# A 32x32 triangular solve fed by block transposes on VectorE in place of trips through DRAM

## The chip, the cores and the metric

The kernel runs on one core of one Trainium2 chip. The metric is the device time of one execution in microseconds; of several executions the median is taken. The engines are TensorE (PE, with its weight loads as PEld), VectorE (DVE), ScalarE (ACT), GpSimd (POOL) and SyncE (SP). SyncE, ScalarE and GpSimd also issue DMAs.

## The reference

One decoder block on 1024 tokens with 1024 channels: an RMS norm, one wide input projection, two token mixers side by side (a mixture of three dilated sliding-window attentions, and a gated DeltaNet), SiLU and sigmoid gates, an output projection, the residual and a last norm. The change lies in the DeltaNet mixer, which works on 8 heads with chunks of 64 tokens:

```python
k_beta = kc * bc[..., None]
a = jnp.einsum('bhnid,bhnjd->bhnij', k_beta, kc) * decay_strict
eye = jnp.eye(c, dtype=a.dtype)
t_inv = lax.linalg.triangular_solve(eye + a, jnp.broadcast_to(eye, a.shape),
                                    left_side=True, lower=True, unit_diagonal=True)
u = t_inv @ (vc * bc[..., None])
w = t_inv @ (k_beta * jnp.exp(G)[..., None])
```

So for each head and each chunk a unit lower triangular matrix of 64x64 is inverted: 8 heads x 16 chunks = 128 matrices. The inverses give u and w, which a scan over the chunks then uses. All of this is in float32.

## The kernel before

**What fills the time.** Most of the work is the projections. They are cut into units of weight columns (attention, DeltaNet, gate, up), and each unit is a generator that issues three float16 matmuls per step (lines 183 to 185). A class `Feed` holds the units. TensorE's order is written out by hand: the code of a stage issues its own small matmuls and calls `feed.tick(n)` between them, and each tick puts one step of a unit into TensorE's queue. So TensorE always has projections to do while another engine prepares the next small step. If a small step is not ready when TensorE comes to it, TensorE waits, because its queue runs in order.

**The other engines.** The order of VectorE, ScalarE, GpSimd and SyncE is not written by hand. A planner lays it out ahead of time by priorities and by its own estimates of durations, and each engine then runs its queue in that fixed order. `tc.high_priority()` moves instructions ahead (evictions of PSUM banks), and the solve is traced with an offset of `-SOLVE_LATER` (1500), so that it is put behind other work and fills gaps. Weight loads are DMAs that GpSimd issues (`load_w`, line 162). ScalarE makes the high half of each weight block (line 166), and VectorE the low half (line 83, `wlo`).

**Buffers.** Tiles with the same tag share their buffers. In the pool `p2_` the tags `As`, `X` and `T1p` have one buffer each. Tag `As` holds As, T1 and later a load of `kbt`; tag `X` holds X and later another load of `kbt`; tag `T1p` holds T1p and also the staging tile `kd` of `spill_keys`.

**The solve.** The heads are worked in two groups `hb` of four. For each group a tile `MT[hb]` of [128, 8, 2, 2, 64] holds 32 pairs (n) of 64x64 matrices: 128 partitions are two chunks of 64 rows, so four blocks `kb` of 32 rows, and b = kb % 2 says which half of a chunk. The diagonal 32x32 blocks are inverted by substitution on VectorE, and TensorE's `merge` makes the off-diagonal block from them. The steps:

- `keys_side(hb)` (lines 1275 to 1303) normalises the keys, packs two scale vectors into `pack`, forms the products of the keys in `pairs` (the results go to `MT[hb]`), and calls `spill_keys`. Then it writes the four diagonal blocks of `MT` to a DRAM tile `m_d`, with rows and matrices exchanged. It transposes `pack` on TensorE (line 1294), copies it on ScalarE, and sends it through DRAM to `bsc`, one scale vector per matrix.
- `solve(hb)` (lines 1305 to 1337) loads `As` from `m_d`, so that each of the 128 partitions holds one 32x32 block (partition = kb, n). VectorE scales it, and 31 steps of two instructions each build the inverse in `X`. `T1` is minus X with its two block indices exchanged. `X` and `T1` go to DRAM (`u_d`, `t_d`) and come back with partitions exchanged: `X` into the diagonal blocks of `MT[hb]`, and `T1` into `T1p`.
- `merge(hb)` (lines 1339 to 1382) has TensorE multiply `T1p` with the off-diagonal block (line 1350), VectorE scale the result to Y, and TensorE multiply by the other diagonal block (line 1365); ScalarE copies that back to `MT` (line 1372). `MERGE_TICKS` = 5 ticks stand between the parts.
- `state_parts(hb)` loads `rvt` and `kbt` and forms u and w (lines 1413 and 1417).

The order is: `decay`, `keys_side` and `solve` of group 0, the same of group 1, then `state_side(0)` (merge and state of group 0), the query pairs of group 0 (line 1266), `state_side(1)`, and the query pairs of group 1. After them comes the scan over the chunks (from line 1672), which starts near 781 us.

Of the kernel before, what the change touches and what calls it, by code (L numbers as in the profile page):

```python
# [77 lines left out]
def hybrid_block(ctx: ExitStack, tc: tile.TileContext, A):  # L78
# [1097 lines left out]
    def heads_h2(x):  # L1176
        return x.rearrange("p t (q e) -> p t e q", e=2)
# [97 lines left out]
    def keys_side(hb):  # L1275
        hsl = slice(4 * hb, 4 * hb + 4)
        sumsq(hb, kT, kss, keep_keys)
        rnorm(rk[:, :, hsl], kss, 1.0)
        TT(brk[:, :, hsl], rk[:, :, hsl], beta[:, :, hsl], ALU.mult)
        TT(bgk[:, :, hsl], brk[:, :, hsl], eG[:, :, hsl], ALU.mult)  # L1280
        pack = p2_.tile([128, 2, 8, 4], F32, name="pack", tag="pack", bufs=2)
        packs.append(pack[:, 0].rearrange("p t h -> p (t h)"))
        for i, x in enumerate((brk, rk)):
            V.tensor_copy(pack[:, i].rearrange("p t (e q) -> p t e q", e=2), heads_h2(x[:, :, hsl]))
        pairs(hb, kT, MT[hb])
        spill_keys(hb)
        m_d = tc.dram_tile([4, 32, 32, 32], F32, name=f"m_d{hb}")
        for kb in range(4):
            b = kb % 2
            nc.sync.dma_start(out=m_d[kb].rearrange("n j i -> j n i"),  # L1290
                              in_=MT[hb][32 * kb:32 * kb + 32].rearrange("p t e q i -> p (t e q) i")[:, :, 32 * b:32 * b + 32])
        feed.tick(4)
        pp = bank("G", 2)
        PE.transpose(pp[0:64, 0:128], pack.rearrange("p a t h -> p (a t h)"), ident)
        packT = p2_.tile([64, 128], F32, name="packT", tag="packT", bufs=1)
        SC.copy(packT, pp[0:64, 0:128])
        sc_d = tc.dram_tile([2, 4, 32, 32], F32, name=f"sc_d{hb}")
        for i in range(2):
            nc.sync.dma_start(out=sc_d[i].rearrange("k n i -> n k i"),
                              in_=packT[32 * i:32 * i + 32].rearrange("p (k i) -> p k i", i=32))  # L1300
        bsc = p2_.tile([128, 2, 32], F32, name="bsc", tag="bsc", bufs=2)
        nc.sync.dma_start(out=bsc, in_=sc_d.rearrange("a k n i -> (k n) a i"))
        return m_d, bsc

    def solve(hb, m_d, bsc):

        As = p2_.tile([128, 32, 32], F32, name="As", tag="As", bufs=1)
        nc.sync.dma_start(out=As.rearrange("p j i -> p (j i)"), in_=m_d.rearrange("k n j i -> (k n) (j i)"))
        TT(As, As, bsc[:, 0, None, :].to_broadcast([128, 32, 32]), ALU.mult)
        TT(As, As, bsc[:, 1, :, None].to_broadcast([128, 32, 32]), ALU.mult)  # L1310
        X = p2_.tile([128, 32, 32], F32, name="X", tag="X", bufs=1)
        GP.memset(X, 0.0)
        GP.memset(X.rearrange("p a b -> p (a b)")[:, ::33], 1.0)
        for k in range(31):
            n = 31 - k
            tmp = p2_.tile([128, 256], F32, name="stmp", tag="stmp", bufs=1)
            tv = tmp[:, :(k + 1) * n].rearrange("p (a b) -> p a b", b=n)
            TT(tv, As[:, k:k + 1, k + 1:].to_broadcast([128, k + 1, n]),
               X[:, :k + 1, k:k + 1].to_broadcast([128, k + 1, n]), ALU.mult)
            TT(X[:, :k + 1, k + 1:], X[:, :k + 1, k + 1:], tv, ALU.subtract)  # L1320
        TT(X, X, bsc[:, 1, None, :].to_broadcast([128, 32, 32]), ALU.mult)
        T1 = p2_.tile([128, 32, 32], F32, name="T1", tag="As", bufs=1)
        V.tensor_scalar(T1, X.rearrange("p j i -> p i j"), -1.0, None, op0=ALU.mult)
        u_d = tc.dram_tile([4, 32, 32, 32], F32, name=f"u_d{hb}")
        t_d = tc.dram_tile([4, 32, 32, 32], F32, name=f"t_d{hb}")
        nc.sync.dma_start(out=u_d.rearrange("k n j i -> (k n) (j i)"), in_=X.rearrange("p j i -> p (j i)"))
        nc.sync.dma_start(out=t_d.rearrange("k n j i -> (k n) (j i)"), in_=T1.rearrange("p j i -> p (j i)"))
        U = MT[hb]
        T1p = p2_.tile([128, 8, 4, 32], F32, name="T1p", tag="T1p", bufs=1)
        for kb in range(4):  # L1330
            b = kb % 2
            if b == 0:
                nc.sync.dma_start(out=T1p[32 * kb:32 * kb + 32].rearrange("p t h j -> p (t h) j"),
                                  in_=t_d[kb].rearrange("n i j -> i n j"))
            nc.sync.dma_start(out=U[32 * kb:32 * kb + 32].rearrange("p t e q i -> p (t e q) i")[:, :, 32 * b:32 * b + 32],
                              in_=u_d[kb].rearrange("n j i -> j n i"))
        return T1p

    def merge(hb, T1p, bsp):
# [121 lines left out]
    for hb in range(2):  # L1461
        decay(hb)
        side.append(keys_side(hb))
        with tc.high_priority(offset=-SOLVE_LATER):
            solved.append(solve(hb, *side[hb]))
    feed.until(("gdn", 1, 2))
    feed.tick(M_LAG)

# [532 lines left out]
```

## Time and profile before

| | us |
|---|---|
| median of 3 runs | 1077.93 (1072.84 to 1079.19) |
| the profiled execution | 1078.95 |
| its span | 1077.2 |
| TensorE busy | 1049.5 |
| VectorE busy | 864.0 |
| ScalarE busy | 559.2 |
| GpSimd busy | 56.1 |

Times in the profile are us from the start of the span unless marked ns. The busy rows cut the span into 40 equal slices of about 27 us and give tenths of busy time. PEclk is the clock that TensorE was granted, in tenths of full speed. In a timeline a row gives start, duration, engine, line, operation and its operands, the count (xN), and in brackets the idle time before it and what ended it. "SPq", "POOLq" and "ACTq" are DMA issues in those queues. Matmuls overlap, so the duration of one is longer than the step from one start to the next. Line numbers of helpers (83, 86) cover many operations, which are told apart by the tile names.

### The profile page before, as it was taken

To read this page: it belongs to the slowest core of one execution; us is meant where nothing else is said; L and a number is where in the kernel's file an instruction comes from. 1 tells how busy PE (TensorE), PEld (TensorE's weight loads), DVE (VectorE), ACT (ScalarE), POOL (GpSimd) and SP (SyncE) were. 2 spreads that over 40 slices of the span, in tenths; PEclk is the share of its full clock that TensorE was granted. 3 is DMA by queue.
4 is the path that set the end of the run, shared out by engine and by line. 5 is a ranking of instruction groups with operands and counts; after the bars stand their busy time and mean duration, and the time that the engine had idled before them with its cause. 6 is when DMAs were issued, how large, how long until landed. Compare 5 with 4: busy or idle time off the path is not lost.

```text
span 1077.2 us, 23669 instructions
## 1 busy us (share of the span) xinstructions
PE 1049.5 (97%) x9398; PEld 639.4 (59%) x9398; DVE 864.0 (80%) x1982; ACT 559.2 (52%) x1272; POOL 56.1 (5%) x107
## 2 busy tenths in 40 slices
PE   7999999999999999999999999998999999999997
PEld 5995685775956755766645545544545555444443
DVE  6997997879878779979966997985588778889934
ACT  6455766567565666557645623243454345333622
POOL 0000000000000000000000001110200000000000
PEclk9999999999999999999999999998999999999999
DMA  7144531633626332641235258784685533753231
GB/s 277 61 133 103 139 104 61 161 100 94 173 70 163 102 102 65 177 110 49 77 118 170 79 139 208 228 254 139 204 264 164 148 98 124 267 193 121 79 118 78
DMA packets 99488, 148.47 MB, mean 138 GB/s; under 512 B 31136, under 2 KB 64416, under 8 KB 98224
## 3 DMA queue, kind: packets, MB, share of 16 engines
q1 hardware_dynamic: 68976, 84.60, 27.4%
q0 software_dynamic: 12320, 44.11, 13.8%
q10 hardware_dynamic: 18080, 18.23, 4.9%
q8 instruction: 74, 1.21, 0.5%
q14 instruction: 38, 0.31, 0.1%
HBM read 91.13 MB, written 36.90 MB: 119 GB/s over the span
## 4 chain that ended last, share of the span: by engine, by line
PE 51%; DVE 31%; DMA 8%; ACT 4%; issue 3%; SPq 2%; DVEq 0%; ACTq 0%
PE ps_mm L183 13%; PE ps_mm L185 12%; PE ps_mm L184 12%; DVE ca L83 3%; DVE wlo L83 3%; DVE rt L86 2%; DVE X L86 2%; DVE stmp L86 2%; DVE sm L799 2%; DVE tl L86 1%; PE ps_G L813 1%; SPq L629 1%; DMA wos<-in_w_out 1%; ACT sm L803 1%; DVE rx L86 1%
## 5 line engine op out<-in xcount | busy, mean ns | idle before, releaser
L185 PE MATMUL ps_mm<-h_hi,wlo 128*128 128x512 f16 (+1 forms) x552 | 208.3, 377 | 0.0
L183 PE MATMUL ps_mm<-h_hi,whi 128*128 128x512 f16 (+1 forms) x492 | 185.7, 378 | 0.0
L184 PE MATMUL ps_mm<-h_lo,whi 128*128 128x512 f16 (+1 forms) x492 | 185.5, 377 | 0.0
L185 PEld LDWEIGHTS <-wlo 128*128 128x128 f16 x788 | 77.3, 98 | 86.7 <-issue 0.8
L183 PEld LDWEIGHTS <-whi 128*128 128x128 f16 x848 | 83.2, 98 | 69.1 <-issue 0.7
L184 PEld LDWEIGHTS <-whi 128*128 128x128 f16 x848 | 83.1, 98 | 68.7 <-issue 2.4
L183 PE MATMUL ps_mm<-whi,h_hi 128*128 128x256 f16 x384 | 105.1, 274 | 0.0
L184 PE MATMUL ps_mm<-wlo,h_hi 128*128 128x256 f16 x384 | 104.7, 273 | 0.0
L185 PE MATMUL ps_mm<-whi,h_lo 128*128 128x256 f16 x384 | 104.7, 273 | 0.0
L803 ACT ACTIVATE sm<-sm,osb 128x128 f32<-128x128 f32 (+1 forms) x160 | 69.5, 435 | 66.3 <-DVE osb L799 59.9
L86 DVE TENSOR_TENSOR tl<-ps_G,th 128x256 f16<-128x256 f32 (+1 forms) x96 | 51.9, 541 | 21.1 <-ACT th L818 20.6
L83 DVE SCALAR_TENSOR_TENSOR wlo<-wstage,whi 128x1024 f16<-128x1024 f32 x50 | 60.9, 1219 | 3.4 <-ACT whi L166 3.2
L799 DVE CUSTOM_DVE_ANT_0 sm<-ps_S,amask 128x128 f32<-128x128 f32 (+1 forms) x192 | 59.2, 346 | 5.1 <-PE ps_S L792 5.0
L83 DVE SCALAR_TENSOR_TENSOR ca<-xc,cw,ca 128x512 f32<-128x512 f32 x72 | 53.8, 747 | 5.6 <-ACT ca L1010 4.8
L166 ACT ACTIVATE whi<-wstage 128x1024 f16<-128x1024 f32 x49 | 51.4, 1051 | 2.0 <-ACT gst L948 0.8
L83 DVE SCALAR_TENSOR_TENSOR whi<-wstage,whi 128x512 f16<-128x512 f32 x60 | 40.8, 687 | 13.6 <-ACT whi L330 12.9
L813 PE MATMUL ps_G<-cons,sm 128*128 128x128 f32 x280 | 47.9, 275 | 2.3 <-DVE tl L86 1.2
L330 ACT ACTIVATE whi<-wstage 128x512 f16<-128x512 f32 x60 | 37.1, 626 | 19.0 <-DVE wstage L329 13.9
L184 PEld LDWEIGHTS <-h_hi 128*128 128x128 f16 x384 | 45.8, 119 | 1.6
L183 PE MATMUL ps_mm<-h_hi,wlo 128*128 128x512 f16 x120 | 45.6, 380 | 1.0 <-DVE rx L83 1.0
L183 PEld LDWEIGHTS <-h_hi 128*128 128x128 f16 x384 | 45.6, 119 | 1.5
L185 PEld LDWEIGHTS <-h_lo 128*128 128x128 f16 x384 | 45.5, 119 | 1.4
(445 smaller groups left out, 2579.7 us busy)
## 6 DMA issues: line engine op xcount, KB each, us to landing
wstage<-in_w POOLq DMA_DIRECT2D x68, 512.0 KB, 4.8
og<-osb ACTq DMA_DIRECT2D x32, 132.0 KB, 2.1
og<-og SPq DMA_DIRECT2D x32, 132.0 KB, 2.2
gspb<-gst ACTq DMA_DIRECT2D x16, 256.0 KB, 2.1
sga<-gspa SPq DMA_DIRECT2D x8, 512.0 KB, 7.1
wstage<-in_w_up POOLq DMA_DIRECT2D x8, 512.0 KB, 5.2
wos<-in_w_out SPq DMA_DIRECT2D x8, 512.0 KB, 5.7
sgb<-gspb SPq DMA_DIRECT2D x8, 512.0 KB, 5.8
```

The lines of the kernel that those rows point to most:

```text
L83: (eng or V).scalar_tensor_tensor(out, in0, scalar, in1, op0=op0, op1=op1)
L86: (eng or V).tensor_tensor(out, in0, in1, op)
L166: in_turn(SC.activation(hi[:, 4 * c:4 * c + 4], st, AF.Copy, scale=W_SCALE))
L183: PE.matmul(out, lhsT=wh(k), rhs=mh(k), start=first and i == 0, stop=False, skip_group_check=True)
L184: PE.matmul(out, lhsT=wh(k), rhs=ml(k), start=False, stop=False, skip_group_check=True)
L185: last_pe[0] = PE.matmul(out, lhsT=wl(k), rhs=mh(k), start=False, stop=last and i == len(ks) - 1, skip_group_check=True).ins.name
L330: in_turn(SC.activation(t[:, b, 0], self.part[name], AF.Copy, scale=W_SCALE))
L629: nc.sync.dma_start(out=dst[r0:r0 + 32, hd], in_=pt[name[1]][32 * hd:32 * hd + 32, "AB".index(name[0])])
L799: V.tensor_tensor_reduce(P[:, u, :128 * nk], psc[:, u * 256:u * 256 + 128 * nk], mask, -cexp, -NEG, ALU.add, ALU.min, accum_out=osb[:, 256 ...
L803: SC.activation(P[:, u, :128 * nk], P[:, u, :128 * nk], AF.Exp, bias=osb[:, 256 + hd:257 + hd], scale=-1.0, accum_out=osb[:, 260 + hd:261 ...
L813: PE.transpose(pt[:, c:c + 128], P[:, u, i * 128:i * 128 + 128], ident)
```

## The change

The four trips of a group through DRAM are replaced. `pack` is transposed in 32x32 blocks on VectorE straight into `bsc`. The four diagonal blocks of `MT` are copied by ScalarE into a contiguous tile `M` (tag X), and VectorE transposes `M` in 32x32 blocks into `As`. After the substitution VectorE transposes `X` once into `T1p` and once into `C` (tag As), and ScalarE copies the four blocks of `C` back into `MT`. The transposes read and write views in which neighbouring elements lie 32 elements apart, except for the reads of `X` for `T1p`. The sign that `T1` carried is moved into the first scale vector of `pack`, so the substitution adds instead of subtracting. TensorE's transpose of `pack` and ScalarE's copy of it are gone, and with them the PSUM bank that they used. `T1p` is now filled in all four row blocks instead of two.

```diff
         for i, x in enumerate((brk, rk)):
-            V.tensor_copy(pack[:, i].rearrange("p t (e q) -> p t e q", e=2), heads_h2(x[:, :, hsl]))
+            V.tensor_scalar(pack[:, i].rearrange("p t (e q) -> p t e q", e=2), heads_h2(x[:, :, hsl]),
+                            (-1.0, 1.0)[i], None, op0=ALU.mult)
         pairs(hb, kT, MT[hb])
         spill_keys(hb)
-        m_d = tc.dram_tile([4, 32, 32, 32], F32, name=f"m_d{hb}")
-        for kb in range(4):
-            b = kb % 2
-            nc.sync.dma_start(out=m_d[kb].rearrange("n j i -> j n i"),
-                              in_=MT[hb][32 * kb:32 * kb + 32].rearrange("p t e q i -> p (t e q) i")[:, :, 32 * b:32 * b + 32])
+        bsc = p2_.tile([128, 2, 32], F32, name="bsc", tag="bsc", bufs=2)
+        V.transpose(bsc.rearrange("p a i -> p (a i)"), pack.rearrange("p a t h -> p (a t h)"))
         feed.tick(4)
-        pp = bank("G", 2)
-        PE.transpose(pp[0:64, 0:128], pack.rearrange("p a t h -> p (a t h)"), ident)
-        packT = p2_.tile([64, 128], F32, name="packT", tag="packT", bufs=1)
-        SC.copy(packT, pp[0:64, 0:128])
-        sc_d = tc.dram_tile([2, 4, 32, 32], F32, name=f"sc_d{hb}")
-        for i in range(2):
-            nc.sync.dma_start(out=sc_d[i].rearrange("k n i -> n k i"),
-                              in_=packT[32 * i:32 * i + 32].rearrange("p (k i) -> p k i", i=32))
-        bsc = p2_.tile([128, 2, 32], F32, name="bsc", tag="bsc", bufs=2)
-        nc.sync.dma_start(out=bsc, in_=sc_d.rearrange("a k n i -> (k n) a i"))
-        return m_d, bsc
+        return bsc
+
+    def diagonal(hb):
+        flat = MT[hb].rearrange("p t e q i -> p (t e q) i")
+        return [(slice(32 * kb, 32 * kb + 32), flat[32 * kb:32 * kb + 32, :, 32 * (kb % 2):32 * (kb % 2) + 32])
+                for kb in range(4)]
 
-    def solve(hb, m_d, bsc):
+    def solve(hb, bsc):
 
+        M = p2_.tile([128, 32, 32], F32, name="M", tag="X", bufs=1)
+        for r, block in diagonal(hb):
+            SC.copy(M[r], block)
         As = p2_.tile([128, 32, 32], F32, name="As", tag="As", bufs=1)
-        nc.sync.dma_start(out=As.rearrange("p j i -> p (j i)"), in_=m_d.rearrange("k n j i -> (k n) (j i)"))
+        V.transpose(As.rearrange("p j i -> p i j"), M.rearrange("p n i -> p i n"))
         TT(As, As, bsc[:, 0, None, :].to_broadcast([128, 32, 32]), ALU.mult)
...
-            TT(X[:, :k + 1, k + 1:], X[:, :k + 1, k + 1:], tv, ALU.subtract)
+            TT(X[:, :k + 1, k + 1:], X[:, :k + 1, k + 1:], tv, ALU.add)
         TT(X, X, bsc[:, 1, None, :].to_broadcast([128, 32, 32]), ALU.mult)
-        T1 = p2_.tile([128, 32, 32], F32, name="T1", tag="As", bufs=1)
-        V.tensor_scalar(T1, X.rearrange("p j i -> p i j"), -1.0, None, op0=ALU.mult)
-        u_d = tc.dram_tile([4, 32, 32, 32], F32, name=f"u_d{hb}")
-        t_d = tc.dram_tile([4, 32, 32, 32], F32, name=f"t_d{hb}")
-        nc.sync.dma_start(out=u_d.rearrange("k n j i -> (k n) (j i)"), in_=X.rearrange("p j i -> p (j i)"))
-        nc.sync.dma_start(out=t_d.rearrange("k n j i -> (k n) (j i)"), in_=T1.rearrange("p j i -> p (j i)"))
-        U = MT[hb]
         T1p = p2_.tile([128, 8, 4, 32], F32, name="T1p", tag="T1p", bufs=1)
-        for kb in range(4):
-            b = kb % 2
-            if b == 0:
-                nc.sync.dma_start(out=T1p[32 * kb:32 * kb + 32].rearrange("p t h j -> p (t h) j"),
-                                  in_=t_d[kb].rearrange("n i j -> i n j"))
-            nc.sync.dma_start(out=U[32 * kb:32 * kb + 32].rearrange("p t e q i -> p (t e q) i")[:, :, 32 * b:32 * b + 32],
-                              in_=u_d[kb].rearrange("n j i -> j n i"))
+        V.transpose(T1p.rearrange("p t h j -> p j (t h)"), X)
+        C = p2_.tile([128, 32, 32], F32, name="C", tag="As", bufs=1)
+        V.transpose(C.rearrange("p n i -> p i n"), X.rearrange("p j i -> p i j"))
+        for r, block in diagonal(hb):
+            SC.copy(block, C[r])
         return T1p
```

More of the change, by code (lines that the diff above doesn't have):

```diff
@@ L1464, in hybrid_block @@
         with tc.high_priority(offset=-SOLVE_LATER):
-            solved.append(solve(hb, *side[hb]))
+            solved.append(solve(hb, side[hb]))
     feed.until(("gdn", 1, 2))
```

## The prediction

> **What bounds the kernel now.** I read the page's first two parts first, then the table by stretches, TensorE's waits, and last the timeline of the stretch where TensorE stops. The page's busy row of TensorE and its clock row:
>
> ```profile
> span 1077.2 us, 23669 instructions
> ...
> PE 1049.5 (97%) x9398; PEld 639.4 (59%) x9398; DVE 864.0 (80%) x1982; ACT 559.2 (52%) x1272; POOL 56.1 (5%) x107
> ...
> PE   7999999999999999999999999998999999999997
> ...
> PEclk9999999999999999999999999998999999999999
> ```
>
> TensorE is the bound: it is idle for 1077.2 - 1049.5 = 27.7 us in all, and its busy row and its clock row drop together in one slice in the middle. The page's matmuls overlap, so a 9 only says that no gap is visible. The table by stretches (busy time and count of PE, PEld, DVE, ACT, POOL, then clock, DMA share, GB/s) shows where the idle time lies:
>
> ```profile
> 560.00:729.00 169.00, 169.00 (x1667) 89.11 (x1666) 139.60 (x273) 71.45 (x121) 15.54 (x28) 1.00 0.63 176
> 729.00:741.00 12.00, 8.01 (x85) 4.49 (x83) 5.88 (x11) 3.93 (x9) 0.54 (x1) 0.72 0.75 213
> 741.00:1060.00 319.00, 318.05 (x2901) 157.35 (x2900) 241.57 (x502) 136.88 (x264) 15.97 (x29) 1.00 0.48 156
> 1060.00:1077.00 17.00, 9.46 (x55) 4.74 (x53) 6.64 (x15) 4.39 (x13) 0.00 (x0) 0.92 0.16 63
> ```
>
> Everything that the change touches starts near 580 us. From there to 729 TensorE has no gap, in 729 to 741 it idles for 12.00 - 8.01 = 4.0 us, and from 741 to 1060 for 319.00 - 318.05 = 0.95 us in all. Its waits name the first:
>
> ```profile
> PE ps_S L1350 <- DMA T1p<-t_d: 4.0, 1, 4.0
> ```
>
> That is the merge of the second group of heads, waiting for a block that the solve sent through DRAM. The chain of waits gives the trip, and TensorE's timeline what it costs:
>
> ```profile
> 709.96 1.24 DVE X L86
> 711.26 5.01 DMA u_d<-X
> 716.66 1.50 SPq L1335
> 719.29 2.99 SPq L1335
> 722.33 11.21 DMA T1p<-t_d
> ...
> 729.35 0.24 PE L1350 MATMUL ps_S<-T1p,MT 32*32 32x32 f32 x2
> 733.58 1.91 PE L1350 MATMUL ps_S<-T1p,MT 32*32 32x32 f32 x62 [3.99 <-DMA T1p<-t_d]
> 735.42 0.61 PE L183 MATMUL ps_mm<-h_hi,whi 128*128 128x512 f16 x1
> 735.82 0.63 PE L184 MATMUL ps_mm<-h_lo,whi 128*128 128x512 f16 x1
> ...
> 739.92 0.38 PE L183 MATMUL ps_mm<-h_hi,whi 128*128 128x512 f16 x1
> 740.14 0.38 PE L184 MATMUL ps_mm<-h_lo,whi 128*128 128x512 f16 x1
> ...
> 745.87 1.20 PE L1365 MATMUL ps_G<-MT,Y 32*32 32x32 f32 x64
> 747.00 0.39 PE L183 MATMUL ps_mm<-h_hi,whi 128*128 128x512 f16 x1
> ```
>
> The second solve's last product is done at 709.96 + 1.24 = 711.2, and its merge can run only at 733.6: over 22 us in DRAM and in SyncE's queue. TensorE arrives at 729.35.
>
> **What the stall costs.** Between 729.35 and 739.92 TensorE ran the 64 small matmuls of one half merge, nine wide matmuls and four 128x128 transposes. At full clock the wide ones step by 740.14 - 739.92 = 0.22 us; 64 small ones take 747.00 - 745.87 = 1.13 us; the four transposes, 512 columns in all, I price at two wide steps, since no row here times them apart: 0.44. That is 1.13 + 9 x 0.22 + 0.44 = 3.55 us, and it took 739.92 - 729.35 = 10.57. So the stall costs **7.0 us**: 4.0 of waiting and 3.0 because the clock is halved afterwards (the wide step at 735.42 is 0.40, the stretch's mean clock 0.72). The clock loss goes with the wait, since the rows around show clock 1.00. Behind it TensorE has next to no gap until 1060, so the 7.0 us pass to the end; what is late next is the feed of matmuls itself, and then the tail, which the change does not touch.
>
> **The change, part by part.** Its prices come from these rows (VectorE, ScalarE, TensorE, SyncE and GpSimd; in rows with three numbers, min/median/max in ns):
>
> ```profile
> L1323 DVE TENSOR_SCALAR T<-X x2: 1053/1056/1058, 644.9 to 711.2; 128x1024 f32<-128x1024 f32 x2
> 609.61 0.18 DVE L86 TENSOR_TENSOR stmp<-As,X 128x31 f32<-128x31 f32 x1
> 643.13 0.21 DVE L86 TENSOR_TENSOR stmp<-As,X 128x31 f32<-128x31 f32 x1
> 584.30 0.17 DVE L1284 COPY pack<-brk 128x32 f32<-128x32 f32 x1
> L166 ACT ACTIVATE whi<-wstage 128x1024 f16<-128x1024 f32 x49 | 51.4, 1051 | 2.0 <-ACT gst L948 0.8
> 589.90 0.27 PE L1294 MATMUL ps_G<-cons,pack 128*64 128x128 f32 x1
> 590.01 0.38 PE L183 MATMUL ps_mm<-h_hi,whi 128*128 128x512 f16 x1
> 663.51 0.56 SPq L1308 DMA_DIRECT2D As<-m_d x1
> 647.68 0.95 POOL L1312 MEMSET X<- 128x1024 f32 x1 [17.62 <-DMA u_d<-X]
> 648.57 0.53 POOL L162 DMA_DIRECT2D wstage<-in_w  x1
> ```
>
> TensorE loses two transposes of the pack, 590.01 - 589.90 = 0.11 us each: **0.2 us**, directly on the bound. The sign flips (multiply by -1 in place of a copy, add in place of subtract) are the same kind of operation on the same size, nothing.
>
> VectorE gains per head group three 32x32-block transposes over 128x1024 and a small one, and loses T1. No transpose is in this trace. The lower bound is T1 itself, which reads the same tile in the same strided order: 1.06 us. The upper: the first and the last step of the solve have 31 elements each, the first side by side, the last 128 bytes apart, and the last takes 0.03 us more, 1 ns an element; 1024 strided elements would cost 1.0 us more, 2.1 in all. I take 2.0, because most of these views are strided on both sides. Per group that is 3 x 2.0 + 0.2 (nearest: the pack copy at 0.17) - 1.06 = 5.1, for both 10 us (with the lower bound 4.6). It hides in the 169.0 - 139.6 = 29.4 us in which VectorE idles before 729; the solve is deferred work, planned into gaps.
>
> [...]
>
> ScalarE gains eight copies per group, 32 partitions by 1024 elements. Nearest row: 1.05 us for 1024 elements; 16 x 1.05 = 17 us. It hides in 169.0 - 71.5 = 97.5 us of idle ScalarE. If that cover fails, the evictions queued behind a copy on ScalarE wait 1 us each, and TensorE has three banks, each filled by 24 wide matmuls in 24 x 0.22 = 5.3 us, ahead of them.
>
> SyncE's queue loses all DMAs of the solve: 16 of them per group (four for m_d, two for sc_d, one each for bsc, As, u_d and t_d, two for T1p, four for MT). What stood behind them (key and value spills) can only come earlier.
>
> GpSimd: the memset of X now waits until M, which shares X's buffer, has been transposed. Behind it wait weight loads: the second memset stood 17.6 us at the head of GpSimd's queue, and the load behind it went out 0.9 us after it. Both wait on the second solve's start now.
>
> Does the second merge get ready in time? In the trace the second solve's input load was only issued at 663.51. Now its input needs X of the first group back (T1 of the first solve ended near 646, plus at most two transposes more), four copies, one transpose: about 655 to 660, some ten us sooner. Even with no start gained: 711.2, plus 2.0 (first transpose), plus 4.0 (two transposes), plus 4.2 to 8.4 (four copies, alone or taking turns with evictions) gives 721.4 to 725.6, before 729.35. So the stall goes whole, and the merge then stands 4 to 19 us ahead.
>
> **Sum.** The profiled execution took 1078.95 us: the span of 1077.2 and 1.75 around it. 1078.95 - 7.0 - 0.2 = **1071.8 us**. The median of the runs is 1077.93, 1.0 below the profiled execution; one run took 1072.84, which would fit a run that mostly escaped this stall, so against the median I expect about 6 us, 0.6%.
>
> **The rivals.**
>
> *Stall in another place.* The planner lays out VectorE's, ScalarE's and GpSimd's queues anew, and the orders are then fixed. A transpose of 2 us or a copy in front of an urgent eviction can hold TensorE, most easily in the merges, which give VectorE only five feed steps of three wide matmuls, 5 x 3 x 0.22 = 3.3 us, for a Y that takes 1.4:
>
> ```profile
> 735.52 1.41 DVE L86 TENSOR_TENSOR Y<-ps_S,pack 32x512 f32<-32x512 f32 x2 [1.25 <-PE ps_S L1350]
> ```
>
> For it: VectorE is over 80% busy there. Against: no TensorE wait of this kind is in 560 to 729, although the solve's own full-size products already stood there. A new stall just like the old one costs the same 7.0: 1078.8; one of 1 to 3 us, with the clock held, leaves 1073 to 1075. [...]
>
> *Slower: ScalarE waits at the head of its queue.* The copies of the second group's blocks cannot start until the first group's X has been transposed for the last time, around 650. If the plan puts them earlier in ScalarE's order than the chip gets there, all evictions behind them wait. Up to about 10 us late (two full banks) TensorE doesn't notice; from there each us is lost, plus 3.0 for the clock, so it decides from some 24 us on (1071.8 + 14 + 3.0 = 1088.8). At 32 us late, about the length of one substitution: 1071.8 + 22 + 3.0 = 1097. Against it: the order on GpSimd came from the same plan, and there the memset that waited for this very point held the load behind it by only 0.9 us.
>
> *Much faster.* From 580 on TensorE's idle time outside the tail is 4.0 + 0.95 us, with 3.0 of clock and 0.2 of transposes 8.2 in all: 1078.95 - 8.2 = 1070.8 is the floor by this trace. A gain over 1% needs 4 us more from gaps that the pipelined matmuls hide, and would come out near 1066.
>
> **From cases to numbers.** Forecast 0.63 (own range 1069 to 1074.5); a stall elsewhere 0.20 (1074.5 to 1080); slower 0.10; much faster 0.07. The range, 1067.5 to 1080, takes in the first two and the spread of a few us among the runs. One per cent is about what a measurement of this kernel can tell: faster means below 1067.2, slower above 1088.7. The forecast and the stall elsewhere both lie between these, so the same has 0.63 + 0.20 = 0.83, faster 0.07, slower 0.10.
>
> **What would show it.** [...] Wrong: a clock drop anywhere after 580; a ScalarE wait of many us on a transpose with PSUM evictions behind it; a late weight load behind the memset; or the time unchanged although the wait is gone, which would mean that TensorE's gapless feed hides another limit.

## The result: 1.4% slower

Five runs of the changed kernel took 1091.37 to 1093.96 us, median **1092.40**; five of the kernel before had a median of 1077.71. The ratio is **1.0141, 95% interval 1.0129 to 1.0153**. The prediction was 1071.8 us, and its bound for "slower" was 1088.7: it was wrong on the sign.

The profiled execution of the changed kernel took 1093.16 us. The page's span, its busy times, TensorE's busy row and the clock row:

```profile
span 1091.4 us, 23646 instructions
PE 1050.2 (96%) x9396; PEld 638.6 (59%) x9396; DVE 872.9 (80%) x1988; ACT 575.6 (53%) x1286; POOL 56.2 (5%) x107
PE   7999999999999999999999998989999999999997
PEclk9999999999999999999999998999999999999999
```

Between the first slice and the last, two slices of the busy row are below 9 where one was; the first of them has the lower clock, three slices earlier than before. The table by stretches over the part that the change touches, first of the kernel before, then of the changed one (length, then busy time and count of PE, PEld, DVE, ACT, POOL, then clock, DMA share, GB/s):

```profile
560.00:820.00 260.00, 256.01 (x2942) 136.41 (x2941) 199.24 (x392) 111.82 (x193) 24.66 (x44) 0.99 0.63 182
```

```profile
560.00:820.00 260.00, 242.90 (x2748) 128.51 (x2746) 194.92 (x367) 121.22 (x196) 24.77 (x44) 0.99 0.46 150
```

TensorE idled 260.00 - 256.01 = 4.0 us there, and now 260.00 - 242.90 = 17.1 us. Those 13.1 us are most of the span's 1091.4 - 1077.2 = 14.2. The DMA share fell from 0.63 to 0.46, as the change says it should, and bought nothing. The waits of TensorE in the changed kernel, all of this stretch but for smaller ones (matmul's output, line, what it waited for, us in all, times, longest):

```profile
PE ps_O L1427 <- DVE rv L86: 5.4, 1, 5.4
PE ps_mm L183 <- ACT ca L1010: 3.9, 1, 3.9
PE ps_G L1352 <- DVE Y L86: 2.3, 3, 1.3
PE ps_G L1195 <- ACT cth L1024: 1.8, 1, 1.8
PE ps_S L1266 <- ACT uw L1411: 1.3, 1, 1.3
PE ps_S L1404 <- DMA kbt<-kb_d: 1.3, 1, 1.3
```

The merge's wait for T1p is gone. Six others have come, and none of them is for an operation that the change added: they are for old evictions, products and loads (`rv` is the value chunk that VectorE takes out of the one bank ps_O; `ca` is the convolution's accumulator) which now run later. TensorE's rows behind the longest wait show that it costs more than its 5.4 us:

```profile
669.58 1.08 PE L1427 MATMUL ps_O<-cons,vT 128*128 128x128 f32 x4 [5.40 <-DVE rv L86]
670.46 0.63 PE L183 MATMUL ps_mm<-h_hi,whi 128*128 128x512 f16 x1
...
674.30 0.55 PE L183 MATMUL ps_mm<-h_hi,whi 128*128 128x512 f16 x1
674.69 0.38 PE L184 MATMUL ps_mm<-h_lo,whi 128*128 128x512 f16 x1
```

Four transposes and ten wide matmuls took 674.69 - 669.58 = 5.11 us, which at the full clock's step of 0.22 would be 0.44 (the prediction's estimate for the four) + 10 x 0.22 = 2.6: 2.5 us more. The granted clock was 0.50 there from 669.5 to 674, and 1.00 from 675 on. So the old stall of 4.0 + 3.0 was traded for one of 5.4 + 2.5 further up, and five others beside it.

How that first stall is made is seen in the queues of ScalarE and VectorE ahead of it (start, duration, what; in brackets the idle time before it and what ended that). ScalarE of the changed kernel:

```profile
651.92 3.15 ACT L1323 COPY MT<-C 32x1024 f32<-32x1024 f32 x3 [5.75 <-DVE C L1321]
...
656.38 0.72 ACT L1021 ACTIVATE vT<-ca 128x256 f32<-128x256 f32 x2
657.00 1.04 ACT L166 ACTIVATE whi<-wstage 128x1024 f16<-128x1024 f32 x1
...
660.18 2.10 ACT L1302 COPY M<-MT 32x1024 f32<-32x1024 f32 x2
...
663.04 1.04 ACT L1302 COPY M<-MT 32x1024 f32<-32x1024 f32 x1
664.11 0.59 ACT L1008 COPY xc<-ps_mm 128x512 f32<-128x512 f32 x1
```

and VectorE:

```profile
658.08 1.23 DVE L83 SCALAR_TENSOR_TENSOR wlo<-wstage,whi 128x1024 f16<-128x1024 f32 x1 [2.70 <-ACT whi L166]
...
664.73 0.17 DVE L1007 COPY xc<-xc 128x3 f32<-128x3 f32 x1 [3.19 <-ACT xc L1008]
...
666.90 1.99 DVE L1304 STREAM_TRANSPOSE As<-M 128x1024 f32<-128x1024 f32 x1
668.79 0.64 DVE L86 TENSOR_TENSOR rv<-ps_O,bg 128x512 f32<-128x512 f32 x1
```

Three copies of C hold the head of ScalarE's queue for 5.75 us, waiting for VectorE; the value eviction vT, the weight rounding whi and the later xc stand behind them and behind the copies into M. VectorE waits 2.70 and 3.19 us for whi and xc, and then does the second solve's transpose before the rv for which TensorE has been idle since 664.2. That reading names three suspects: ScalarE's copies, VectorE's transposes, and the place of the second solve. The experiments take them apart.

### The profile page after: what moved, and what is told of

The parts are those of the page before. It is cut to its first block, busy times and chain, and to the rows that moved or that the text cites. A ratio compares the mean times of both kernels' runs of the same rounds, so it can differ in the third digit from the quotient of the medians.

```text
span 1091.4 us, 23646 instructions
## 1 busy us (share of the span) xinstructions
PE 1050.2 (96%) x9396; PEld 638.6 (59%) x9396; DVE 872.9 (80%) x1988; ACT 575.6 (53%) x1286; POOL 56.2 (5%) x107
## 4 chain that ended last, share of the span: by engine, by line
PE 58%; DVE 26%; ACT 6%; DMA 4%; issue 4%; SPq 2%; POOL 0%; ACTq 0%; DVEq 0%
PE ps_mm L183 14%; PE ps_mm L185 13%; PE ps_mm L184 13%; DVE ca L83 3%; DVE wlo L83 2%; DVE X L86 2%; DVE stmp L86 2%; PE ps_S L185 2%; PE ps_S L183 2%; PE ps_S L184 2%; DVE sm L799 2%; DVE tl L86 1%; PE ps_G L813 1%; SPq L629 1%; DVE rt L86 1%
## 5 line engine op out<-in xcount | busy, mean ns | idle before, releaser
L813 PEld LDWEIGHTS ps_G<-cons,sm 128*128 128x128 f32 x280 | 35.5, 141 | 19.6 <-ACT sm L803 5.1
```

Of the source, the lines that this page charges most:

```text
L813: PE.transpose(pt[:, c:c + 128], P[:, u, i * 128:i * 128 + 128], ident)
```

## Experiments: copies or transposes alone, half the change alone

The first four kernels took away one kind of work or one side of the solve. In the first, ScalarE's copies and the buffer M are left out (the transposes read and write a fixed half of MT's blocks, so half of the blocks are the wrong ones); in the second the six large transposes are left out (T1p is filled by one strided pass of VectorE, and the values are wrong).

```diff
 e1_no_copies
-        for r, block in diagonal(hb):
-            SC.copy(M[r], block)
-        V.transpose(As..., M.rearrange("p n i -> p i n"))
+        V.transpose(As..., flat.rearrange("p n i -> p i n"))      # flat: MT[hb], first half of each block
...
-        V.transpose(C..., X...)                                   # and the four copies of C
+        V.transpose(flat..., X...)
 e2_no_transposes
-        V.transpose(As..., M...)
-        TT(As, As, bsc[:, 0, None, :]..., ALU.mult)
+        TT(As, M, bsc[:, 0, None, :]..., ALU.mult)
...
-        V.transpose(T1p..., X)
-        V.transpose(C..., X...)
+        V.tensor_scalar(T1p..., X..., 1.0, None, op0=ALU.mult)
-            SC.copy(block, C[r])
+            SC.copy(block, X[r])
 e3_front_only: way in by copies and transposes, way out through DRAM
 e3_back_only:  way in through DRAM, way out by transposes and copies
```

> Left out: the 16 ScalarE copies; VectorE transposes the first 32 columns of each matrix straight out of and into MT, so for half of the row blocks it is the wrong block that is inverted (the amount of VectorE work is the same). With the copies goes the buffer M. Theory A (the copies on ScalarE, 16 x 1.04 us, hold the evictions of the conv units, and TensorE's waits of 5.4 and 3.9 us come from that): both waits go, 1071 to 1076 us. Theory B (the three 2.0 us transposes per group on VectorE stand in front of urgent evictions): stays at 1087 to 1093. Theory C (the new plan as such, whatever it holds): anywhere between 1075 and 1090, with waits in other places.

> Left out: the six large transposes on VectorE; the solve reads M and ScalarE copies X back without any exchange of partitions, and T1p is filled by one strided VectorE pass of 1.06 us as T1 was (wrong values, same ScalarE work as the changed kernel, VectorE work as in the kernel before). Theory A: the copies still block the evictions, 1085 to 1093 us. Theory B: 1071 to 1076. Theory C: between 1075 and 1090.

> Only the way into the solve is changed (copies into M, one transpose, the scale vectors by a transpose); the way out goes through DRAM as before. Half of the copies (8) and two of six transposes. Theory A: ScalarE has 4 copies in a row at the most, so at most one of the two waits: 1076 to 1084 us, and the wait for T1p of 4 us may be back. Theory B: 1076 to 1084 too. If the way in alone carries the loss, through M in X's buffer: 1085 to 1092.

> Only the way out is changed (two transposes per group and the copies back into MT); the way in goes through DRAM as before, so M doesn't exist. Theory A: 4 copies in a row at the most, no wait of T1p: 1071 to 1078 us. Theory B: four of six transposes remain: 1082 to 1090. Loss through M in X's buffer: 1071 to 1075.

Measured, against a median of before of 1076.93 us: e1 **1087.70** (1.0095, 1.0078 to 1.0112), e2 **1090.78** (1.0128, 1.0113 to 1.0143), e3_front **1089.42** (1.0114, 1.0099 to 1.0130), e3_back **1093.36** (1.0151, 1.0136 to 1.0167).

Neither kind of work alone is the cause: without the copies two thirds of the loss stay, without the transposes nine tenths. The front half loses nearly as much as the whole, the back half a little more, and outside all three ranges expected of it. In all four, TensorE waited 3.5 to 5.5 us at ps_O near 664 us for rv or vT, and in all four the second solve's first instructions stood in front of the last value chunks in VectorE's queue. That gave theory D, so far argued only: without the trip through DRAM the planner, which knows no trip now, puts the second solve's start sooner in the fixed queues, ahead of the value chunks, which on the chip run late. Its rival, E: the transposes and copies behind the first substitution delay the value chunks by themselves.

## Experiments: the place of the second solve

In these the second solve is traced later and its first instruction gets a planning order, no wait on the chip, behind the sixth of the eight rv:

```diff
-            SC.copy(M[r], block)
+            m = SC.copy(M[r], block)
+            if hb:
+                tc.add_manual_dep(m.ins, rvs[5], order_only, reason="behind the value rows")
...
-        with tc.high_priority(offset=-SOLVE_LATER):
-            solved.append(solve(hb, side[hb]))
+        if not hb:
+            with tc.high_priority(offset=-SOLVE_LATER):
+                solved.append(solve(hb, side[hb]))
     feed.until(("gdn", 1, 2))
     feed.tick(M_LAG)
+    with tc.high_priority(offset=-SOLVE_LATER):
+        solved.append(solve(1, side[1]))
 e8_gp_late: the same, SC.copy -> GP.tensor_copy in all 16 copies
 e9_back_late: the same on e3_back_only (its first TT of As carries the order)
 e10_before_idle: the kernel before, and ahead of its T1
+        for _ in range(2):
+            V.transpose(T1.rearrange("p j i -> p i j"), X.rearrange("p j i -> p i j"))
```

> The changed kernel with every transpose and copy kept; only the planner is told that the second solve's copies into M come after the sixth of the eight rv instructions of the value turns (a planning order, no wait on the chip), so that VectorE's queue has the second solve behind the last value chunk, as in the kernel before. Theory D (the second solve's early place in the two fixed queues makes the stall at 664 to 670 us): TensorE's wait for rv, 5.4 us, falls under 2 us and the clock stays at 1.00 there (3.2 us more), so 1082 to 1086; the second merge is ready about 727 to 732 us and waits at most 3 us. Theory E (the two transposes and four copies behind the first substitution make it, wherever the second solve is put): a wait of 3 us or more stays at ps_O, with its drop of the clock, and the time is 1088 to 1093.

> As the run with the second solve put late, and all 16 copies on GpSimd instead of ScalarE: ScalarE's queue is then that of the kernel before. Theory D: 1078 to 1084, the value chunks' vT no more than the 3 us later that VectorE is behind. Theory E with its weight on VectorE: 1086 to 1092; E with its weight on ScalarE's copies: 1078 to 1082, and 4 us or more below the run with the copies on ScalarE. If a GpSimd copy takes much over 2 us, the second merge waits for the last one and the time is 1085 or more by that.

> The way into the solve through DRAM as in the kernel before, the way out by transposes and copies (1093.36 us when the planner was free), now with the second solve's first multiplication planned behind the sixth rv. Theory D: 1083 to 1088. Theory E: 1090 to 1095, since all that it blames is still there.

> The kernel before with two transposes of X more behind each substitution, whose result is overwritten by the T1 that was made there anyway: VectorE has the changed kernel's extra 4 us at that place, and the order around them is the old one. Theory D: 1077 to 1081, no wait of TensorE over 2 us at 660 to 670 us, the second merge's wait 4 us longer at most. Theory E with its weight on VectorE: a wait for rv or vT of 3 us or more at 660 to 670 us, 1084 to 1090.

Measured (before: 1076.97): e7 **1086.67** (1.0093, 1.0069 to 1.0117), e8 **1086.94** (1.0094, 1.0071 to 1.0117), e9 **1086.02** (1.0084, 1.0057 to 1.0111), e10 **1080.95** (1.0046, 1.0028 to 1.0064).

Place is a part, and not all of it. The place alone gives back 5.7 us of the whole change's loss (1092.40 to 1086.67, between the ranges of D and E) and 7.3 of the back half's (1093.36 to 1086.02). But 9 to 10 us stay, e8 missed D's range by 3 us, and the kernel before loses 4.0 us by two transposes behind each substitution, 4.2 us each time, that nothing reads. That loss lies in D's range, and E's large wait did not come. Part of how it arises is seen in the trace: the last value chunk's three accumulations start later by as much as VectorE was given (the kernel before, then with the two idle transposes):

```profile
659.58 2.33 DVE L83 SCALAR_TENSOR_TENSOR ca<-xc,cw,ca 128x512 f32<-128x512 f32 x3 [1.04 <-ACT ca L1010]
```

```profile
645.07 4.19 DVE L1324 STREAM_TRANSPOSE T<-X 128x1024 f32<-128x1024 f32 x2
...
663.70 2.33 DVE L83 SCALAR_TENSOR_TENSOR ca<-xc,cw,ca 128x512 f32<-128x512 f32 x3 [1.05 <-ACT ca L1010]
```

663.70 - 659.58 = 4.1 us, of which TensorE notices 1.7 as a wait for rv. Later follow 1.0 with no cause in the profile, 1.8 for Y, 0.9 for T1p and 0.7 for a qT whose taps stand between the transposes behind the second substitution. Each value chunk goes ScalarE, VectorE, ScalarE, TensorE, VectorE in turn, and four of them follow one another every 4.2 us with ScalarE and VectorE waiting for each other; the idle VectorE of that stretch is inside this chain, not beside it. In e9 the same row starts at 663.91 and TensorE's wait for rv is 2.6 us; in e7, where the first substitution also ends 3 us later, it starts at 667.62 and the wait is 2.5. In e8 TensorE does not wait at ps_O at all, but that does not clear or blame ScalarE's copies: waits for gm, 4.7 us near 600, made it come there 4.1 us later than in e7 (668.28 against 664.2).

## Experiments: the four quarters one by one

The change has four quarters that can be made alone: each head group's way in and way out. All else is the kernel before (`e11_in1`: first group's way in, and so on; the DRAM code stands in an `else`).

```diff
+        if hb:                     # e11_out2; e11_out1 has "if not hb:"
+            V.transpose(T1p..., X)
+            V.transpose(C..., X...)
+            for r, block in diagonal(hb):
+                SC.copy(block, C[r])
+        else:
             ... T1, u_d, t_d and their DMAs as before
```

> The kernel before with one quarter of the change: the first solve's way in by copies into M and transposes (bsc too), everything else through DRAM. The second solve keeps its old place behind the third of its four rv. Theory D and E (place of the second solve; work between the first substitution and the value chunks) both have nothing here but a first substitution that ends 3 us later: the changed kernel's two short waits at 580 to 620 us, 2.6 us together, and the old wait for T1p with its clock drop, 1079 to 1082. Rival F (the old order fits its work and any change of the plan loses about 1%): 1085 to 1090.

> The kernel before with the first solve's way out alone by two transposes and four copies. C's buffer is free sooner than the stored T1's was, and the planner puts the second solve's first two multiplications in front of the value chunks' last ca and rv. Theory D with E: the stall for rv at 660 to 675 us with its drop of the clock, 8 to 10 us lost, a second solve that is ready sooner so that the T1p wait shrinks, 1082 to 1090. Rival F: 1085 to 1090, not told apart here.

> The kernel before with the second solve's way in alone by copies and a transpose. No extra work lies behind the first substitution, but the second solve stands in front of two chunks' ca and rv in VectorE's queue. Theory D: TensorE waits for rv 3 us or more at 660 to 672 us, 1080 to 1088 with the second merge's wait shorter than 4.0 us. Theory E: no such wait, 1072 to 1078.

> The kernel before with the second solve's way out alone by two transposes and four copies: the only place where TensorE waited for the trip through DRAM. The queues of VectorE and ScalarE are those of the kernel before up to the end of the second substitution. By the reading so far (the loss came from the other three quarters): the T1p wait of 4.0 us goes and the clock stays at 1.00, up to 3.0 us more, so 1070 to 1074. Rival F: 1080 or more, through a wait behind 716 us (ScalarE's copies of C in front of xc and ca, or un_d queued behind a burst of loads).

Measured (before: 1077.34): in1 **1080.06** (1.0020, 1.0008 to 1.0031), out1 **1088.89** (1.0100, 1.0084 to 1.0117), in2 **1084.58** (1.0064, 1.0046 to 1.0082), out2 **1079.11** (1.0016, 1.0004 to 1.0027).

No quarter gains. The first group's way in costs its two small waits. The first group's way out and the second group's way in each make the stall at ps_O by themselves, and together they make it only once, which fits that the quarters add up to 2.0% and the whole loses 1.4%. In out1 the second solve's start moved because C gives its buffer (shared with As) back sooner than the T1 that had to be stored; in in2 because M needs no DMA (both are read from the code and the queues, not tried). TensorE's largest wait in out1 and then in in2:

```profile
PE ps_O L1454 <- DVE rv L86: 5.4, 1, 5.4
```

```profile
PE ps_O L1459 <- ACT vT L1021: 3.6, 1, 3.6
```

The most telling quarter is out2. It removes the one wait for DRAM that TensorE had, and up to that point all queues are the old ones. Its waits:

```profile
PE ps_G L1379 <- DVE Y L86: 1.8, 2, 1.3
PE ps_G L1266 <- ACT qT L1021: 1.3, 1, 1.3
PE ps_S L1266 <- ACT qT L1021: 1.1, 1, 1.1
...
PE ps_O L1247 <- DVE rq L1251: 0.8, 1, 0.8
```

5.0 us of others in place of 4.0, with a drop of the clock among them (0.91 at 740 to 760 us): the expected 7.0 us gain is gone, and no queue was laid out worse ahead of it. The qT waits have two sources. VectorE's taps of that chunk start behind both transposes, and on ScalarE three copies of C stand in front of the eviction of qT:

```profile
715.02 2.30 DVE L83 SCALAR_TENSOR_TENSOR ca<-xc,cw,ca 128x512 f32<-128x512 f32 x3
```

```profile
715.15 3.15 ACT L1334 COPY MT<-C 32x1024 f32<-32x1024 f32 x3 [3.64 <-DVE xc L1007]
718.33 0.63 ACT L1021 ACTIVATE qT<-ca 128x512 f32<-128x512 f32 x1
```

In the kernel before, that eviction ran 3.7 us sooner:

```profile
714.62 0.63 ACT L1021 ACTIVATE qT<-ca 128x512 f32<-128x512 f32 x1 [3.22 <-DVE ca L83]
```

The taps end at 715.02 + 2.30 = 717.3, where those of the kernel before ended at 714.6; so 2.7 of the 3.7 us are VectorE's transposes, and 1.0 the copies.

## Experiments: the same work in idle gaps, and what is left

The last four ask whether amount or place of the work decides. In the two e12 kernels the second way out stands behind accumulations (taps) at whose end VectorE had been idle; `taps` holds the instruction of each chunk's last tap. e13_in2_late is e11_in2 with the second solve behind the sixth rv; e13_late_gpback is e7_late with C's eight copies on GpSimd.

```diff
 e12_gaps_gp, e12_gaps_act (on e11_out2; traced after feed.tick(Q_LAG[0]))
         i = V.transpose(T1p.rearrange("p t h j -> p j (t h)"), X)
+        tc.add_manual_dep(i.ins, taps[0, 0, 1, 0], order_only, reason="behind the taps")
         i = V.transpose(C.rearrange("p n i -> p i n"), X.rearrange("p j i -> p i j"))
+        tc.add_manual_dep(i.ins, taps[0, 0, 1, 1], order_only, reason="behind the taps")
         for r, block in diagonal(hb):
-            SC.copy(block, C[r])
+            GP.tensor_copy(block, C[r])      # e12_gaps_act keeps SC.copy
```

> As the run with the second way out alone, with its work moved into idle gaps: the first transpose (T1p) is planned behind the three taps at 712 us, the second (C) behind those at 716 us, where VectorE sat idle 1.63 and 1.70 us in the kernel before, and the four copies are GpSimd's (1.43 us each by the run that had all copies there). If place decides: taps at most 0.5 us later than before, no wait for qT over 0.5 us at 715 to 725 us, C in place at about 727 us, ahead of the merge at 729, the clock at 1.00, and 1070 to 1073. If the amount of work decides, or a new wait takes the stall's place whatever is done: 1076 to 1080, as with the work at once (1079.1).

> The same with the four copies on ScalarE, where the planner puts two behind the first weight rounding at about 722 us and two behind the next eviction. If only the transposes' place mattered: 1070 to 1074. If ScalarE's copies in front of evictions cost 1 us each on the path: 1074 to 1078, with waits for xc, ca or qT of 2 us or more in sum at 720 to 740 us.

> The whole change with the second solve put behind the sixth rv (1086.67 us with all copies on ScalarE), and the eight copies of C on GpSimd. ScalarE then rounds the weights (whi) 6 us sooner and VectorE's 2.7 us of idle in front of the second taps goes. If the copies in front of whi and vT carry the rest of the stall for rv: that wait (2.5 us) under 1 us, 1081 to 1084. If not: 1085 to 1088.

> The second solve's way in alone by copies and a transpose (1084.58 us where the planner put it 10 us sooner), now with its copies behind the sixth rv. Theory D (its place): the wait for vT or rv at 660 to 675 us (3.6 us and a clock of 0.91) goes altogether, the wait for T1p through DRAM comes back with 4 to 7 us and its clock drop, and the time is 1076 to 1081. Theory E has nothing behind the first substitution here and so gives no account of the 3.6 us; if that wait stays, both are wrong.

Measured (before: 1077.50): e12_gaps_gp **1077.72** (1.0008, 0.9999 to 1.0017), e12_gaps_act **1076.01** (0.9991, 0.9982 to 1.0000), e13_late_gpback **1088.40** (1.0111, 1.0097 to 1.0124), e13_in2_late **1077.48** (1.0006, 0.9995 to 1.0017).

**Place of the second solve.** e13_in2_late settles it: the same copies and the same transpose cost 7.1 us more ahead of the value chunks (1084.58) than behind them (1077.48, as fast as the kernel before within its interval). Its stall at ps_O is gone. The wait for T1p did not come back with 4 to 7 us, as expected, but with 0.3.

**The second way out.** In gaps, it costs nothing in sum, and e12_gaps_act is the fastest kernel of this study, by about 0.1%, with an interval that reaches up to 1.0000. It is no gain to speak of, though the stall is wholly gone, the qT waits too. TensorE in e12_gaps_act around the merge, which now starts with no wait:

```profile
730.31 1.20 PE L1373 MATMUL ps_S<-T1p,MT 32*32 32x32 f32 x64
...
735.30 0.66 PE L1250 MATMUL ps_O<-cons,qT 128*128 128x128 f32 x4 [1.74 <-DVE rq L1254]
...
738.73 0.21 PE L1388 MATMUL ps_G<-MT,Y 32*32 32x32 f32 x1 [1.31 <-DVE Y L86]
...
739.46 0.25 PE L1388 MATMUL ps_G<-MT,Y 32*32 32x32 f32 x1 [0.48 <-DVE Y L86]
```

In place of the 4.0 us stand 1.74 + 1.31 + 0.48 = 3.5 us within 10 us, as waits for rq (the sums of squares of q, out of the same single bank) and for Y, with a lower clock behind them (0.93 at 740 to 760). The two differ in origin.

The wait for Y is what TensorE's stall seems to have covered. In e10, e11_out2, both e12 kernels and e13_in2_late, whose waits for T1p were 0 to 0.9 us, the second merge waited 1.8 to 1.9 us for Y; in the kernel before and in e11_in1, whose waits for T1p were 4.0 and 3.2, it did not.

The wait for rq is, by the traces, the price of the copies. In the kernel before, rq was done at 730.86 + 0.69 = 731.55, and without its stall TensorE would have asked for it at about 729.35 + 1.13 + 9 x 0.22 = 732.5 (an estimate from the prediction's rows). In e12_gaps_act TensorE comes to the merge 1.0 us later, but rq 3.7, because ScalarE's xc ahead of it, at 724.96 in the kernel before, stands behind two copies of C (rq in the kernel before; then ScalarE and rq in e12_gaps_act):

```profile
730.86 0.69 DVE L1251 TENSOR_REDUCE rq<-ps_O 128x8 f32<-128x512 f32 x1 [0.59 <-ACT ps_O L1250]
```

```profile
727.00 2.09 ACT L1359 COPY MT<-C 32x1024 f32<-32x1024 f32 x2
729.12 0.58 ACT L1010 COPY xc<-ps_mm 128x512 f32<-128x512 f32 x1
```

```profile
734.55 0.69 DVE L1254 TENSOR_REDUCE rq<-ps_O 128x8 f32<-128x512 f32 x1 [0.59 <-ACT ps_O L1253]
```

In e12_gaps_gp, with no copies on ScalarE, the wait for rq is 1.5 us: there two of VectorE's taps beside GpSimd's copies took 2.80 us in place of 1.54.

**Copies on GpSimd** came with longer VectorE work in both runs. e13_late_gpback has C's first copies on GpSimd, and its VectorE beside them:

```profile
652.55 3.48 POOL L1325 COPY MT<-C 32x1024 f32<-32x1024 f32 x2 [18.23 <-DVE C L1323]
```

```profile
653.45 1.03 DVE L1007 COPY xc<-xc 128x3 f32<-128x3 f32 x1
654.40 3.73 DVE L83 SCALAR_TENSOR_TENSOR ca<-xc,cw,ca 128x512 f32<-128x512 f32 x3
```

The three taps took 3.73 us where they take 2.33 in the kernel before, and a copy of three columns 1.03 where it takes 0.19 in the changed kernel. So this run does not tell what ScalarE's copies alone cost in the whole change; that stays open. Open, too, is the second large wait of the changed kernel (ps_mm for ca, 3.9 us): in its trace ScalarE waits 3.9 us for the buffer of a uw whose DMA is under way, while loads of kbt and rvt that SyncE could issue only from 719.6 us on fill the DMA engines (share 0.97 from 722 to 725). It is read from the trace and was not tried by itself.

## Why the prediction was wrong, step by step

**Durations were right.** Against 2.0 us for a large transpose, 0.2 for the small one and 1.05 for a copy, the tiles' rows of the changed kernel (ns, min/median/max):

```profile
L1304 DVE STREAM_TRANSPOSE As<-M x2: 1993/2047/2101, 604.0 to 666.9; 128x1024 f32<-128x1024 f32 x2
```

```profile
L1323 ACT COPY MT<-C x8: 1040/1042/1047, 651.9 to 724.5; 32x1024 f32<-32x1024 f32 x8
```

The transposes lie within the bounds 1.06 to 2.1, at the upper end; T1p's took 1.95. The small one took 0.24. The busy time of VectorE grew by 8.9 us and that of ScalarE by 16.4, against the 10 and 17 forecast.

**"About 655 to 660, some ten us sooner" failed, and with the wrong sign.** The prediction counted the second solve's earlier start as margin. The planner did put it earlier, but on the chip M's last copy ended at 666.5 and the first multiplication began at 670.02, against 669.08 before: in order, it was ahead of two value chunks, and in time it came no sooner. This place costs 5.7 to 7.3 us (e7, e9, e13_in2_late, each against its pair).

**"It hides in the 29.4 us in which VectorE idles" failed.** e10 gave VectorE 4.2 us behind each substitution, in that idle time, and lost 4.0 us. The idle time was real, but lay between links of a chain that alternates between ScalarE and VectorE. The same holds of the 97.5 us of ScalarE: C's copies waited 5.75 us at the head of its queue with vT and whi behind them, and even in e12_gaps_act two of them made rq late. The slower rival had this very mechanism, but let it decide only from 24 us on, since TensorE "has three banks" ahead of it. That is true of the projections; the value turns have one bank, ps_O, and there TensorE noticed at once. The 9 to 10 us that stay with the second solve put late were not taken apart further; in e7's trace TensorE waits 2.5 us for rv, 1.9 for Y, 1.9 for qT and 1.8 for cth.

**"The 7.0 us pass to the end" failed too.** The stall did go, and the price of 7.0 us for it was sound: four transposes, priced at 0.44, took 670.46 - 669.58 = 0.88 in the changed kernel at a granted clock of 0.50. But "what is late next is the feed of matmuls itself" was read from rows in which TensorE had just stood still for 4.0 us. What is late next is Y, by 1.8 us in the kernels named above. With the work placed best (e12_gaps_act), where the copies add 1.7 us for rq, about 1.5 us of the 7.0 arrive, in an interval that reaches down to 0. No run takes the stall away without adding work, so how much would arrive then stays open.

**The rivals.** "Stall in another place" had the right cause (a transpose or a copy in front of an urgent eviction), named merges where the value turns were hit, and was priced as one stall of at most 7.0 us; it was one of 5.4 + 2.5, one of 3.9 and several of 1 to 2. It also priced a stall of 1 to 3 us "with the clock held", which no run shows in general: the clock held behind waits of 1.73 us (e10) and 2.69 (e13_late_gpback) and fell with one of 2.59 (e9_back_late), where nine wide matmuls took 667.32 - 663.69 = 3.6 us in place of 9 x 0.22 = 2.0. **The smaller terms:** GpSimd's memset waited 13.3 us for the transposes of M in all, and no wait of TensorE leads back to it. SyncE's queue did not come out only earlier: a load of kbt stood 18.3 us at its head, until the transpose into C had read X, whose buffer it takes, and the next one 4.5 us, until C had been copied out.

## What to carry to other kernels

Idle time of an engine covered new work here only where it lay outside a chain of engines that wait for each other (e10: 4.2 us of work behind each substitution, in VectorE's idle time, cost 4.0); follow the nearest urgent buffer with one bank backward before calling work hidden. Where a planner fixes queue orders ahead of time, taking a latency away can move work up in the order, and what it is moved past decides (here the second solve, 5.7 to 7.3 us): ask for that as for a new wait. And a stall may be what lets the next stages run without gaps, so price its removal by what those stages would show 4 us sooner: here Y (1.8 us), not rq.

## Hardware behaviour that was not expected

**The clock.** In these runs the length of a wait alone did not decide the clock's fall. In the kernel before, the clock was halved behind a wait of 3.99 us (steps of 0.40 to 0.43). In the changed kernel it stayed at full speed after an idle 3.89 us (a step of 0.21, a granted clock of 1.00 from 731 to 736):

```profile
731.21 0.38 PE L183 MATMUL ps_mm<-h_hi,whi 128*128 128x512 f16 x1 [3.89 <-ACT ca L1010]
731.42 0.38 PE L184 MATMUL ps_mm<-h_lo,whi 128*128 128x512 f16 x1
```

In e9_back_late it fell after a wait of only 2.59 us, and in the midst of work, 663.69 - 663.01 = 0.7 us after TensorE had started again:

```profile
663.01 0.63 PE L1443 MATMUL ps_O<-cons,vT 128*128 128x128 f32 x4 [2.59 <-DVE rv L1447]
663.47 0.38 PE L183 MATMUL ps_mm<-h_hi,whi 128*128 128x512 f16 x1
663.69 0.57 PE L184 MATMUL ps_mm<-h_lo,whi 128*128 128x512 f16 x1
...
667.03 0.45 PE L183 MATMUL ps_mm<-h_hi,whi 128*128 128x512 f16 x1
667.32 0.38 PE L184 MATMUL ps_mm<-h_lo,whi 128*128 128x512 f16 x1
```

The step is 0.22 us from 663.47 to 663.69 and 0.42 to 0.43 from 664.05 on, with a mean granted clock of 0.84 from 664 to 674. The clock came back in the matmul at 667.03, 3.3 us after it fell in the one at 663.69. In e13_late_gpback TensorE waited 2.69 us for an rv, longer than in e9_back_late, and the steps behind it stayed at 0.21 to 0.22, with a granted clock of 1.00 from 664 to 674. What decides the fall is not shown by these runs.

**GpSimd beside VectorE.** In e13_late_gpback GpSimd's four copies of 32x1024 ran from 652.55 to 656.03 and from 656.56 to 659.04. VectorE's three taps of that stretch took 3.73 - 2.33 = 1.4 us more than in the kernel before, and the three-column copy 1.03 - 0.19 = 0.8 us more than in the changed kernel, while the weight rounding wlo that started ahead of them at 652.34 took 1.22, as in the changed kernel. The runs do not show why.
